# Splitting numbers into two parts: the second part on VectorE alone instead of VectorE or GpSimd

## The chip, the cores and the metric

The kernel runs on one core of a Trainium2 chip. Its time is the device time of one execution in microseconds (us); lower is better. Three runs of the kernel before took 1108.18, 1108.98 and 1110.24 us, so its median is 1108.98 us. In the profile, PE is TensorE's matmuls, PEld its weight loads, DVE is VectorE, ACT is ScalarE, POOL is GpSimd and SP is SyncE, which issues most DMAs.

## What is computed

The reference is a decoder of two layers on one sequence of 1024 positions with 1024 features, in float32. Layer A is gated linear attention; layer B is attention over three dilated windows with shared keys and values. Cut to what matters:

```python
# layer A
q, k, v, g, a_lr = split(x @ w_in)                # 1024 x 3088 weights
log_a = log_sigmoid(a_lr @ w_a2 + b_a2) / 16
o = gla_chunked(q, k, v, log_a)                   # 4 heads, decayed states
o = o * rsqrt(mean(o * o) + eps) * norm_g
x = layer_norm(alpha * x + (o * silu(g)) @ w_out)
# layer B
k, v = split(x @ w_kv); k = rope(k, pos)
q, g = split(x @ w_in); q = rope(q, pos)          # 3 groups x 8 heads of 128
o = softmax-weighted sum over (window, dilation) in ((128,1), (512,4), (2048,16))
x = layer_norm(alpha * x + (o * silu(g)) @ w_out)
```

## The kernel before

**Two parts for each number.** The large products run in TensorE's float32r type, which keeps less of a number than float32. So each operand is held as a high part (a copy rounded to float32r, made on ScalarE by `split_hi`) and a low part (the number less its high part, made by `split_lo`). A product then takes three matmuls: high by high, high by low, low by high. `split_lo` is thus called for every weight and every activation that such a product reads. In the names of the profile `wf` is a weight as loaded, `wh` and `wl` its parts; `woh` and `wol` are those of the last output weights; `xh`, `xl`, `x1h`, `x1l`, `ogh`, `ogl` are parts of activations (of the input, of layer A's result, of the gated attention output); `T` or `tT` are quarter sums of activations and hold both parts.

**Pair jobs.** Most projections of q, k and the queries of layer B go through `pairs` (L777 to L880): two 128-column blocks of weights are multiplied with the activations by a scheme of seven half-size products, P1 to P7, instead of eight. It needs sums of weights (`sum`, with parts in `wh`, `wl` and `s`) and sums of activations (`T`, `tT`). For each job `seven` (L831) copies P1 and P7 out of the accumulator to `u1` and `u2` on ScalarE, and TensorE may start P2, which goes into P1's accumulator, only behind the first copy. Then VectorE adds P6 to `u1`, `c` is `u1` plus the sum of P7 and P4, and `u2` becomes `u1 + u2` (L873 sends it on). In layer B the four quarters of a job are P2's accumulator, `c`, `u2` and `u1`. Each goes through the rotary embedding (`rope`, L1497): `t1` is the quarter times the cosine (VectorE), `t2` two half copies on ScalarE that swap its halves, then times the sine, and `pair` takes `t1 + t2`. The last two may run on VectorE or GpSimd. There are two buffers for `t2`. Layer B has 14 pair jobs: three for the keys and eleven for the queries; the third is the last for the keys, the eighth that for query heads 4 and 5 in the widest window. `xc` is a copy on ScalarE that belongs to turning layer A's result, which goes on beside these jobs (one or two at a job).

**What sets the order.** No instruction is issued as it is written. The code records operations, and a planner (`order`, L270 on) gives each a place by a list schedule with costs for every engine; all are then issued from one line, L469, which is why every row of the profile has this line. `S.vector` binds an operation to VectorE, `S.vp` leaves it to VectorE or GpSimd, `S.va` to VectorE or ScalarE. For such an operation the planner tries both engines and takes the one with the earlier start; an engine is passed over where a cheaper one is free no later:

```python
                    if any(max(free[q], r) <= st and c < o.cost[o.engs.index(e)] for q, c in zip(o.engs, o.cost)):
                        continue

                    key = (max(st, soft), o.prio)
```

So GpSimd gets an operation where the planner thinks VectorE busy. The planner also takes VectorE and GpSimd operations with two inputs in on-chip memory to exclude each other (`shares_port`, L560). Since every choice moves the times of what follows, a change in one choice moves others, on all engines.

Each engine runs its instructions in the planner's order and waits in that order. GpSimd also issues the DMAs that add a low part of weights by accumulation (the rows `DMA wl<-in_w...`).

## Time and profile before

| | |
|---|---|
| median of 3 runs | 1108.98 us (1108.18 to 1110.24) |
| the profiled execution | 1108.76 us |
| its span, first to last instruction | 1107.0 us |
| mean granted clock of TensorE | 0.996 |
| TensorE busy in 490 to 761 us (layer B's pair jobs) | 268.78 of 271.00 us |
| VectorE busy in 490 to 761 us | 223.07 us |
| GpSimd busy in 490 to 761 us | 108.98 us |
| TensorE busy in 761 to 1000 us (attention) | 238.63 of 239.00 us |

The stages in order: the first projections (to 54 us), layer A's pair jobs (54 to 132), linear attention with its value and gate projections (to 360), its output with the layer norm (to 440), layer B's values (from 422) and pair jobs (490 to 761), attention with the gate projections (to 1010), and the output with the layer norm. A row of a group gives engine, operation, output and inputs, count, then busy time in us and the mean in ns of one, then the idle time of the engine just before and what ended it. A row of the timeline gives the start, the duration (of all that a row merges), the engine, the operation and in brackets the idle time before it. A row of stretches gives the length, the busy time of PE, PEld, DVE, ACT and POOL with their counts, the granted clock, the share of DMA and GB/s.

### The profile page before, as it was taken

Reading aid. Unit: us, or ns where it says so; the run is one execution under the profiler, and the core shown is the slowest. Engines: PE = TensorE matmul, PEld = TensorE weight load, DVE = VectorE, ACT = ScalarE, POOL = GpSimd, SP = SyncE. Lnnn points to the kernel's source line nnn. Section 1 sums busy time; section 2 is a strip of 40 time slices with the busy share of each in tenths; the row PEclk is TensorE's granted clock in tenths of the full one; section 3 lists DMA queues with packets and bytes.
Section 4 is the critical chain, followed back from the end, with each engine's and each line's share of the span. In section 5 each row is a group of like instructions: output and inputs, shape, how many; then the busy total and the mean of one; then the engine's idle time right before and its main releaser. Section 6 shows DMA issues by size and latency. Waiting matters only on the chain.

```text
span 1107.0 us, 20264 instructions
## 1 busy us (share of the span) xinstructions
PE 1093.0 (99%) x7532; PEld 933.5 (84%) x7532; DVE 878.1 (79%) x1756; ACT 651.3 (59%) x1326; POOL 263.1 (24%) x281
## 2 busy tenths in 40 slices
PE   9999999999999999999999999999999999999997
PEld 9988888888888888888878888888888888888876
DVE  5886879999567589887877889885688778896588
ACT  5565545666465265656566666665677787663252
POOL 0122100000013021012454254342233554340010
PEclk9999999999999999999999999999999999999999
DMA  8477773144262455856766686679534552341644
GB/s 298 144 210 207 247 286 120 60 146 168 92 210 87 152 169 183 249 167 154 186 161 180 162 216 168 176 188 277 158 106 124 181 166 91 109 152 68 188 137 171
DMA packets 92626, 185.70 MB, mean 168 GB/s; under 512 B 16912, under 2 KB 38032, under 8 KB 92528
## 3 DMA queue, kind: packets, MB, share of 16 engines
q1 hardware_dynamic: 84320, 167.11, 45.2%
q0 software_dynamic: 8208, 17.31, 9.3%
q8 instruction: 59, 0.97, 0.4%
q14 instruction: 39, 0.32, 0.1%
HBM read 134.57 MB, written 47.71 MB: 165 GB/s over the span
## 4 chain that ended last, share of the span: by engine, by line
PE 94%; DVE 2%; DMA 2%; ACT 1%; issue 1%; POOL 0%; DVEq 0%; ACTq 0%; POOLq 0%
PE acc L469 30%; PE sev L469 28%; PE po L469 11%; PE lv L469 9%; PE vac L469 8%; PE ms L469 4%; PE pro L469 3%; DMA wf<-in_wOB 1%; DMA wf<-in_wB 1%; DVE wl L469 0%; ACT wl L469 0%; DVE rt L469 0%; ACT t L469 0%; ACT wh L469 0%; DVE wol L469 0%
## 5 line engine op out<-in xcount | busy, mean ns | idle before, releaser
L469 ACT ACTIVATE wh<-wf 128x1024 fp32r<-128x1024 f32 (+3 forms) x118 | 99.4, 844 | 91.8 <-PE acc L469 34.6
L469 PE MATMUL sev<-T,wh 128*128 128x512 f32 x448 | 137.9, 389 | 0.0
L469 PEld LDWEIGHTS sev<-T,wh 128*128 128x128 f32 x448 | 84.1, 188 | 17.5
L469 PE MATMUL sev<-T,wl 128*128 128x512 f32 x224 | 87.1, 389 | 0.0
L469 DVE TENSOR_TENSOR wl<-wf,wh 128x1024 fp32r<-128x1024 f32 (+3 forms) x56 | 63.4, 1137 | 10.7 <-ACT wh L469 10.4
L469 PE MATMUL lv<-K,Q 128*64 128x64 f32 (+2 forms) x512 | 71.4, 287 | 0.4 <-DVE sts L469 0.4
L469 PE MATMUL acc<-x1h,wh 128*128 128x512 f32 x160 | 71.1, 444 | 0.0
L469 POOL TENSOR_TENSOR wl<-wf,wh 128x1024 fp32r<-128x1024 f32 x6 | 14.3, 2386 | 228.4 <-PE ms L469 192.4
L469 PE MATMUL acc<-x1h,wl 128*128 128x512 f32 x160 | 62.8, 393 | 0.0
L469 PE MATMUL acc<-x1l,wh 128*128 128x512 f32 x160 | 62.5, 391 | 0.0
L469 DVE CUSTOM_DVE_ANT_0 P<-lv,bmask 128x256 f32<-128x256 f32 (+1 forms) x128 | 47.1, 378 | 15.5 <-PE lv L469 11.9
L469 PEld LDWEIGHTS lv<-K,Q 128*64 128x64 f32 (+1 forms) x512 | 51.6, 164 | 8.9 <-DVE sts L469 1.2
L469 ACT ACTIVATE P<-P,sts 128x64 f32<-128x64 f32 (+2 forms) x128 | 50.0, 392 | 13.2 <-DVE sts L469 12.9
L469 POOL DMA_DIRECT2D wl<-in_wB x42 | 37.0, 888 | 80.5 <-ACT wl L469 78.3
L469 DVE TENSOR_TENSOR u<-u,sev 128x512 f32<-128x512 f32 x54 | 36.7, 684 | 21.4 <-PE sev L469 20.9
L469 POOL TENSOR_TENSOR pair<-t,t 128x512 f32<-128x512 f32 x26 | 43.4, 1672 | 42.7 <-DVE t L469 32.0
L469 PE MATMUL acc<-xh,wh 128*128 128x512 f32 x128 | 52.5, 410 | 0.0
L469 ACT ACTIVATE t<-u 64x512 f32<-64x512 f32 x56 | 35.3, 631 | 28.5 <-DVE u L469 17.7
L469 PE MATMUL acc<-xh,wl 128*128 128x512 f32 x128 | 50.1, 391 | 0.0
L469 PE MATMUL acc<-xl,wh 128*128 128x512 f32 x128 | 50.0, 390 | 0.0
L469 PEld LDWEIGHTS sev<-T,wl 128*128 128x128 f32 x224 | 42.0, 188 | 8.7
L469 PE MATMUL acc<-ogh,wh 128*128 128x512 f32 x120 | 47.4, 395 | 0.0
(347 smaller groups left out, 3431.7 us busy)
## 6 DMA issues: line engine op xcount, KB each, us to landing
wf<-in_wB SPq DMA_DIRECT2D x32, 512.0 KB, 6.4
wf<-in_wA SPq DMA_DIRECT2D x24, 512.0 KB, 4.4
qd<-pair SPq DMA_DIRECT2D x22, 512.0 KB, 4.9
Q<-qd SPq DMA_DIRECT2D x22, 512.0 KB, 6.8
wl<-in_wB POOLq DMA_DIRECT2D x33, 256.0 KB, 7.5
wf<-in_wO SPq DMA_DIRECT2D x16, 512.0 KB, 3.4
wf<-in_wOB SPq DMA_DIRECT2D x16, 512.0 KB, 3.5
wf<-in_wV SPq DMA_DIRECT2D x10, 512.0 KB, 3.4
```

The lines of the kernel that those rows point to most:

```text
L469: getattr(handle[o.eng], meth)(*[conv(a) for a in args], **{k: conv(v) for k, v in kw.items()})
```

## The change

One word changes: `split_lo`'s subtraction is bound to VectorE.

```diff
     def split_lo(dst, src, hi):
-        S.vp.tensor_sub(dst, src, hi.bitcast(F32))
+        S.vector.tensor_sub(dst, src, hi.bitcast(F32))
```

Before, 34 of these subtractions were placed on GpSimd: 7 of 128x1024 (6 `wl`, 1 `wol`) and 27 of 128x512 (7 `wl` of sums, 8 `ogl`, 5 `tT`, 3 `T`, 2 `x1l`, and `s` and `sum`). All are on VectorE now. The planner then places other operations anew. GpSimd has 257 instructions instead of 287, VectorE 1780 instead of 1759, ScalarE 1146 instead of 1137. Twelve of the sums `u2 = u1 + u2` stand on GpSimd, where five did. TensorE has the same matmuls, in an order that differs mostly in the pair jobs of layer B and in the attention stage.

**The third pair job of layer B, on GpSimd and VectorE.** In these names `u1`, `u2`, `c`, `t1`, `t2` and `pair` are the rotary work above, `wl<-sum` a split, and the last number only tells buffers apart. GpSimd before:

```order
L469 TENSOR_TENSOR u2_5849<-u1_5843,u2_5849 128x512
L469 TENSOR_TENSOR t2_5965<-t2_5965,sinT_3181 128x512
L469 TENSOR_TENSOR pair_5984<-t1_5960,t2_5955 128x4x16x8
L469 TENSOR_TENSOR pair_5984<-t1_5963,t2_5965 128x4x16x8
L469 DMA wl_6007<-in_wB 128x512
```

GpSimd now:

```order
L469 TENSOR_TENSOR u2_5860<-u1_5853,u2_5860 128x512
L469 DMA wl_5921<-in_wB 128x512
L469 TENSOR_TENSOR pair_5986<-t1_5965,t2_5949 128x4x16x8
L469 DMA wl_6012<-in_wB 128x512
L469 TENSOR_TENSOR pair_5914<-t1_6002,t2_5996 128x4x16x8
```

VectorE before:

```order
L469 TENSOR_TENSOR u1_5843<-u1_5843,sev_5898 128x512
L469 TENSOR_TENSOR wl_5939<-sum_5816,wh_5926 128x512
L469 TENSOR_TENSOR wl_5939<-sum_5832,wh_5926 128x512
L469 TENSOR_TENSOR c_5948<-u1_5843,sev_5796 128x512
L469 TENSOR_TENSOR t1_5960<-c_5948,cosT_2944 128x512
```

VectorE now:

```order
L469 TENSOR_TENSOR u1_5853<-u1_5853,sev_5855 128x512
L469 TENSOR_TENSOR c_5935<-u1_5853,sev_5802 128x512
L469 TENSOR_TENSOR wl_5956<-sum_5846,wh_5940 128x512
L469 TENSOR_TENSOR wl_5956<-sum_5862,wh_5940 128x512
L469 TENSOR_TENSOR t1_5965<-c_5935,cosT_2944 128x512
```

The sine product of `u2` and one `pair` have left GpSimd, and `c` stands ahead of the two splits instead of behind them. None of the two splits was on GpSimd.

**The eighth pair job of layer B, on GpSimd and ScalarE.** GpSimd before:

```order
L469 TENSOR_TENSOR pair_6800<-t1_6783,t2_6785 128x4x16x8
L469 DMA wl_6807<-in_wB 128x512 x2
L469 TENSOR_TENSOR pair_6860<-t1_6850,t2_6839 128x4x16x8
L469 TENSOR_TENSOR pair_6860<-t1_6873,t2_6866 128x4x16x8
L469 DMA wl_6902<-in_wB 128x512
```

GpSimd now:

```order
L469 TENSOR_TENSOR pair_6800<-t1_6785,t2_6783 128x4x16x8
L469 DMA wl_6810<-in_wB 128x512 x2
L469 TENSOR_TENSOR u2_6749<-u1_6743,u2_6749 128x512
L469 TENSOR_TENSOR t2_6867<-t2_6867,sinT_3181 128x512
L469 TENSOR_TENSOR pair_6886<-t1_6862,t2_6857 128x4x16x8
L469 TENSOR_TENSOR pair_6886<-t1_6865,t2_6867 128x4x16x8
L469 DMA wl_6909<-in_wB 128x512
```

ScalarE now, in the same job:

```order
L469 ACTIVATE t2_6857<-c_6850 64x512 x2
L469 ACTIVATE t2_6867<-u2_6749 64x512 x2
L469 ACTIVATE t2_6894<-u1_6743 64x512
L469 ACTIVATE wh_6902<-wf_6816 128x512
L469 ACTIVATE wl_6909<-wf_6816 128x512
L469 ACTIVATE wh_6902<-sum_6896 128x512
L469 ACTIVATE t2_6894<-u1_6743 64x512
L469 ACTIVATE xc_6922<-xb_6841 128x2x256
L469 ACTIVATE u1_6932<-sev_6853 128x512
```

GpSimd has the order here that it had in the third job before, with `u2` and its sine product. ScalarE's rows are those of the third job before too, where the copy `u1` of the next job stood directly behind the last `t2`; now an `xc` stands between. VectorE makes `c` behind the two splits here, as it did in the third job before. From the start of the next job TensorE has 42 matmuls (P1, P7, P5 and half of P6) ahead of P2, as it had behind the third job before. In the fifth pair job `u2`, its sine product and one `pair` stand on GpSimd now as well, with `c` behind two splits on VectorE, and an `xc` ahead of `u1`; the three splits on ScalarE stand ahead of the last two `t2` copies there, and TensorE has 51 matmuls ahead of P2 of the sixth.

**The first pair job of layer A, on TensorE.** In `tT13` the first digit names the sum (1 for P5, 3 for P7) and the second its piece. Before:

```order
L469 MATMUL sev_783<-tT12_656,wl_754 128x512
L469 MATMUL sev_783<-tT13_781,wh_740 128x512 x2
L469 MATMUL sev_783<-tT13_781,wl_754 128x512
L469 MATMUL sev_768<-tT33_788,wh_524 128x512 x2
L469 MATMUL sev_768<-tT33_788,wl_539 128x512
```

Now:

```order
L469 MATMUL sev_786<-tT12_674,wl_753 128x512
L469 MATMUL sev_769<-tT33_784,wh_523 128x512 x2
L469 MATMUL sev_769<-tT33_784,wl_540 128x512
L469 MATMUL sev_786<-tT13_778,wh_741 128x512 x2
L469 MATMUL sev_786<-tT13_778,wl_753 128x512
```

The last piece of P7 stands ahead of the last piece of P5 now. VectorE makes `tT13` ahead of `tT33` in both.

## The prediction

> **What bounds the kernel now.** I read the head of the profile's page first, then TensorE's own waits, then the time around the longest of them.

> ```profile
> span 1107.0 us, 20264 instructions
> ...
> PE 1093.0 (99%) x7532; PEld 933.5 (84%) x7532; DVE 878.1 (79%) x1756; ACT 651.3 (59%) x1326; POOL 263.1 (24%) x281
> ...
> PE 94%; DVE 2%; DMA 2%; ACT 1%; issue 1%; POOL 0%; DVEq 0%; ACTq 0%; POOLq 0%
> ```

> TensorE is busy 99% of the span and holds 94% of the chain that ended last. VectorE at 79% and GpSimd at 24% are off that chain nearly everywhere. So work that moves from GpSimd to VectorE has no price of its own. It has a price, or a gain, only where TensorE waits for something that the move makes earlier or later. TensorE's waits are these:

> ```profile
> PE sev L469 <- ACT u L469: 2.2, 1, 2.2
> PE lv L469 <- issue: 1.4, 2, 1.1
> PE pro L469 <- DVE zero L469: 1.3, 1, 1.3
> PE vac L469 <- issue: 0.7, 1, 0.7
> PE acc L469 <- POOL wol L469: 0.4, 1, 0.4
> PE lv L469 <- DVE sts L469: 0.4, 1, 0.4
> ```

> They sum to 6.4 us. The waits on "issue" name no engine, and the one on `zero` lies at the start, ahead of every operation that moves. Within reach of the change lie the 2.2 (the fourth pair job waits for a copy that ScalarE makes) and the 0.4 (a split on GpSimd). That bounds any gain: no more than some 3 us of waiting, and what the wait costs after itself. The largest costs more than its row says:

> ```profile
> 556.04 0.62 PE L469 MATMUL sev<-T,wh 128*128 128x512 f32 x2
> 556.50 0.39 PE L469 MATMUL sev<-T,wl 128*128 128x512 f32 x1
> 559.10 0.62 PE L469 MATMUL sev<-x1h,wh 128*128 128x512 f32 x1 [2.22 <-ACT u L469]
> ...
> 562.51 0.51 PE L469 MATMUL sev<-x1h,wl 128*128 128x512 f32 x1
> ```

> ```profile
> 559.10:562.60 3.50, 3.50 (x9) 2.72 (x10) 3.50 (x6) 1.74 (x3) 1.28 (x1) 0.53 0.82 131
> ```

> Matmuls start 0.23 us apart before (two in 556.50 - 556.04). The next should have started at 556.73 and started at 559.10: 2.4 us. Behind the gap the granted clock is 0.53 for 3.5 us, and eight matmuls take 562.51 - 559.10 = 3.41 us where they would have taken 8 x 0.23 = 1.84: another 1.6 us. The stall is worth 4.0 us in all.

> **What makes that stall.** It is the rotary work of the third pair job, on three engines (ScalarE, then GpSimd, then VectorE):

> ```profile
> 549.71 1.27 ACT L469 ACTIVATE t<-c 64x512 f32<-64x512 f32 x2 [3.42 <-DVE c L469]
> 551.01 1.27 ACT L469 ACTIVATE t<-u 64x512 f32<-64x512 f32 x2
> 555.45 0.63 ACT L469 ACTIVATE t<-u 64x512 f32<-64x512 f32 x1 [3.16 <-POOL pair L469]
> ...
> 557.80 0.63 ACT L469 ACTIVATE t<-u 64x512 f32<-64x512 f32 x1
> 558.45 1.09 ACT L469 ACTIVATE u<-sev 128x512 f32<-128x512 f32 x2
> ```

> ```profile
> 546.22 1.61 POOL L469 TENSOR_TENSOR u<-u,u 128x512 f32<-128x512 f32 x1
> 552.43 1.29 POOL L469 TENSOR_TENSOR t<-t,sinT 128x512 f32<-128x512 f32 x1 [4.59 <-ACT t L469]
> 553.68 3.44 POOL L469 TENSOR_TENSOR pair<-t,t 128x512 f32<-128x512 f32 x2
> ```

> ```profile
> 544.68 0.69 DVE L469 TENSOR_TENSOR u<-u,sev 128x512 f32<-128x512 f32 x1 [1.55 <-PE sev L469]
> 545.80 3.19 DVE L469 TENSOR_TENSOR wl<-sum,wh 128x512 fp32r<-128x512 f32 x2 [0.44 <-ACT wh L469]
> 548.92 0.67 DVE L469 TENSOR_TENSOR c<-u,sev 128x512 f32<-128x512 f32 x1
> ```

> Read from the end. TensorE waits for `u<-sev` at 558.45. That copy stands in ScalarE's order behind a `t<-u` that could start only at 555.45, when GpSimd had ended a `pair` and so freed a `t` buffer. That `pair` stood behind GpSimd's product with the sine (552.43), which waited for ScalarE's second `t`. The first `t` waited for `c`, and `c` stood on VectorE behind two splits that took 3.19 us, nearly all of it beside GpSimd's `u` at 546.22. VectorE had been brought into step with TensorE at 544.68 (it waited 1.55 us for it), so lateness from before plays no part: it is the order of this one job that costs 4.0 us.

> **The change, part by part.** Operations that leave GpSimd, and their price on VectorE:

> ```profile
> L469 POOL TENSOR_TENSOR wl<-wf,wh 128x1024 fp32r<-128x1024 f32 x6 | 14.3, 2386 | 228.4 <-PE ms L469 192.4 <-ACT wh L469 36.0
> L469 POOL TENSOR_TENSOR wl<-sum,wh 128x512 fp32r<-128x512 f32 x7 | 9.6, 1374 | 4.9 <-ACT wh L469 4.9
> L469 POOL TENSOR_TENSOR wol<-wf,woh 128x1024 fp32r<-128x1024 f32 x1 | 2.4, 2384 | 48.0 <-ACT woh L469 48.0
> ...
> L469 DVE TENSOR_TENSOR wl<-wf,wh 128x1024 fp32r<-128x1024 f32 x45 | 56.4, 1256 | 9.4 <-ACT wh L469 9.2
> L469 DVE TENSOR_TENSOR wol<-wf,woh 128x1024 fp32r<-128x1024 f32 x7 | 8.6, 1223 | 4.2 <-ACT woh L469 4.2
> ...
> L469 ACT ACTIVATE xc<-xb 128x512 uint16<-128x512 uint16 x16 | 12.6, 786 | 0.4 <-DMA xb<-x1p 0.3
> ```

> Of the 34 splits that move, 7 are 1024 wide and 27 are 512 wide. GpSimd loses 14.3 + 2.4 + 9.6 + 20 x 1.37 = 54 us. VectorE gains 7 x 1.25 + 27 x 0.69 (the row at 544.68) = 27 us, less the 7 sums `u` that the planner now gives to GpSimd in exchange (7 x 0.69 = 5). On VectorE's 878 us that is under 3%, and TensorE waits for VectorE's own results only 0.4 us in the middle of the span, so the 22 us lie beside TensorE's matmuls. If that cover were gone in one place, what is late next is the copy or split that TensorE takes there; the four terms below are those places.

> (a) Third pair job. GpSimd no longer takes the sine product of `u`, nor the second `pair`, and VectorE makes `c` ahead of the two splits. Of the chain above, the 3.19 us ahead of `c` and the 1.29 of the sine go. ScalarE's wait of 3.16 us goes with them, which is more than the stall of 2.4 us: **-4.0 us**. Bounds: 0 (something else is late there) and -4.0.

> (b) Eighth pair job. The order that made the stall stands here now, operation for operation: on VectorE `u`, two splits, then `c`; on GpSimd two DMA issues, `u`, the sine product, `pair`, `pair`; on ScalarE the same `t` copies and splits ahead of the copy for the next job. TensorE has as many matmuls to cover it as at 559 (42 from the next job's start to the product that needs the copy). VectorE is again tied to TensorE by its wait ahead of `u`. So the stall of 4.0 us should come again here, where there is none now. One thing is added: an `xc` copy stands ahead of the `u` copy on ScalarE, 786 ns by its group, some 0.6 us of the queue's time. Behind the waiting ScalarE stand the `u` copies, and TensorE waits for these: **+4.6 us**. Bounds: 0 and 4.6 + 0.8, should `xc` itself wait for its DMA.

> [...]

> (c) The split `wol` near the end goes from 2384 to 1223 ns. TensorE's wait for it, 0.4 us, is shorter than the difference: **-0.4 us** if VectorE is free; 0 if not.

> (d) The first pair job. Five splits of the quarter sums move to VectorE while it makes the last of them for TensorE (VectorE, GpSimd, TensorE):

> ```profile
> 39.23 2.38 DVE L469 TENSOR_TENSOR sum<-wf 128x512 f32<-128x512 f32 x2
> ...
> 53.31 1.29 DVE L469 TENSOR_TENSOR wl<-wf,wh 128x512 fp32r<-128x512 f32 x2 [0.97 <-ACT wh L469]
> ...
> 59.66 1.28 DVE L469 TENSOR_TENSOR tT<-xg,tT 128x512 fp32r<-128x512 f32 x2
> ```

> ```profile
> 39.01 1.45 POOL L469 TENSOR_TENSOR tT<-xg,tT 128x512 fp32r<-128x512 f32 x1 [1.46 <-ACT tT L469]
> ```

> ```profile
> 60.66 0.62 PE L469 MATMUL sev<-tT,wh 128*128 128x512 f32 x2
> ...
> 61.34 0.62 PE L469 MATMUL sev<-tT,wh 128*128 128x512 f32 x2
> ```

> The two splits at 59.66 end at 60.3 and 60.94; TensorE takes the first at 60.66 and the second at 61.34. In the new order TensorE takes the second ahead of the first, so it waits 0.3 us even if VectorE keeps its time. Five more operations cost VectorE 5 x 0.64 = 3.2 us; two sums beside GpSimd's split took 2.38 instead of 1.28, so 1.1 us come back; 0.97 us of idle time is there to be used. Ends: 0 and 0.3 + 3.2 - 1.1 - 0.97 = 1.4. I take **+0.3 us**, near the lower end, because the other three GpSimd splits lay beside VectorE too.

> The sum: 1107.0 - 4.0 + 4.6 - 0.4 + 0.3 = 1107.5. The profiled execution took 1108.76 us, 1.8 over its span, and the median of the runs is 0.2 above that: 1107.5 + 1.8 + 0.2 = **1109.5 us**, 0.5 above 1108.98. About 0.2% (2.2 us) is what a measurement of this kernel can tell from no change.

> **The rivals.** *The stall goes and does not come back* (chance 0.22). If GpSimd's `u` in the eighth job starts after VectorE's two splits, `c` comes some 1.9 us earlier (3.19 against 1.29 for two) and most of the gap closes. Then only (a), (c) and (d) stand: 1107.0 - 4.0 - 0.4 + 0.3 = 1102.9, 1104.9 us. For it: the margin is a matter of which engine starts first. Against it: VectorE's splits wait for ScalarE there (0.44 us), while GpSimd's `u` waits only for VectorE's.

> *Two more waits* (chance 0.21), the side of slower. In the fifth pair job GpSimd now also has `u`, the sine product and a `pair` in a row, and VectorE makes `c` behind two splits. TensorE has 51 matmuls of cover in the sixth job, 9 more than at 559, worth 9 x 0.23 = 2.1 us, and ScalarE has an `xc` copy more. The gap there would be 2.4 + 0.6 - 2.1 = 0.9 us, and 1.6 more if the clock goes down: 2.5 us, 1112.0 us in all. It decides as soon as ScalarE's `u` copy is more than 2.1 us later, relative to its job, than at 558.45. Against it: three copies stand ahead of the wait on GpSimd now, and run while it lasts.

> *The port freed* (chance 0.07). VectorE's operations with two inputs run longer beside GpSimd's, as at 545.80 and 39.23. With 54 us of GpSimd's splits gone, VectorE could be early everywhere, so that each wait within reach and the price of the gap go: 2.4 + 1.6 + 0.4 + 0.4 = 4.8 less, 1104.2 us. Against it: in the eighth job GpSimd's own `u` and `pair` are the neighbours, not splits. [...]

> **How the numbers follow.** The forecast (the stall moves) has 0.50; the rivals 0.22, 0.21 and 0.07. The forecast's own range is 1107.6 (no clock loss in (b), 1.6 less, and 0 for (d)) to 1111.8 (0.8 for `xc`, 0.4 for (c), 1.1 more for (d)). The range reaches to the rivals on both sides: 1104.6 to 1112.6. Faster by over 0.2%: the first and third rivals, 0.29, less what falls short, 0.27. Slower by over 0.2%: the second and the upper end of the forecast, 0.27. Between: 0.46.

> **What would show it.** Right: no wait of TensorE for `u` near 556; one of about 3 us for `u` in the eighth pair job, near 655, with granted clock near 0.5 behind it; no wait for `wol`; GpSimd 30 instructions fewer. Wrong: no wait of TensorE over 1 us between 490 and 761 (first rival), two of them (second), or a change of TensorE's waits in the attention stage behind 761, which no term covers since no split is moved there before 970.

## The result, and the profile after

The changed kernel takes 1115.31 us (median of 6 runs, 1113.10 to 1118.03) against 1108.79 us for the kernel before (median of 6 runs). The ratio is 1.0069, with a 95% interval of 1.0055 to 1.0082: it is slower by 0.7%. The prediction was 1109.5 us with a range up to 1112.6, so the time lies outside the range. The profiled execution took 1115.79 us, with a span of 1114.0 us.

From the page of the changed kernel, the span, the engines' busy time and the chain that ended last:

```profile
span 1114.0 us, 20213 instructions
...
PE 1095.3 (98%) x7532; PEld 935.2 (84%) x7532; DVE 881.5 (79%) x1777; ACT 657.8 (59%) x1335; POOL 218.3 (20%) x251
...
PE 84%; DVE 8%; DMA 3%; ACT 2%; issue 2%; POOL 0%; DVEq 0%; SPq 0%; ACTq 0%; POOLq 0%
```

GpSimd lost 30 instructions and 45 us of work, VectorE gained 3.4 us net, where the prediction reckoned with 22. Summed over VectorE's groups, the operations that it gained are worth 27 us at their mean durations of before, but its operations run shorter now by 21 us in all (`s<-sum,s` took 805 ns on average instead of 1278). That was the premise of the third rival, and it did come true (two splits took 3.19 us beside GpSimd's `u` at 545.80 of the kernel before, and 1.28 at 59.66 with GpSimd idle; what makes them longer is not shown), but TensorE's waits did not go with it. TensorE's share of the chain fell from 94% to 84%, and VectorE, off it before, holds 8%. TensorE has the same 7532 matmuls. Its waits, as total, number and longest:

```profile
PE sev L469 <- ACT u L469: 6.6, 3, 4.6
PE vac L469 <- issue: 2.3, 1, 2.3
PE pro L469 <- DVE zero L469: 1.3, 1, 1.3
PE lv L469 <- issue: 1.1, 2, 0.6
```

The waits for `u` went from 2.2 us in one place to 6.6 in three, and the wait on "issue" at `vac` from 0.7 to 2.3. Since the matmuls are as many, the start of the n-th matmul in the one trace less that in the other tells where the 7.0 us of span came from:

| place | us after less before |
|---|---|
| first 42 us | -0.2 |
| first pair job of layer A, 60 to 65 | +1.1 |
| linear attention, 172 to 218 (3.3 of it at the wait at `vac`) | +3.5 |
| 218 to 490 | -0.3 |
| third pair job of layer B, 559 to 563 | -4.1 |
| eighth, 656 to 668 | +7.9 |
| twelfth, 741 | +1.2 |
| attention | -1.0 |
| `wol` | -0.7 |
| after the last matmul | -0.3 |

The stall of the third pair job is gone and stands in the eighth, as the prediction had it, but twice as large. TensorE there, and then the row of stretches from the wait's end (length, busy time of PE, PEld, DVE, ACT, POOL, then the granted clock):

```profile
656.05 0.39 PE L469 MATMUL sev<-T,wl 128*128 128x512 f32 x1
661.07 0.80 PE L469 MATMUL sev<-x1h,wh 128*128 128x512 f32 x1 [4.63 <-ACT u L469]
...
666.36 0.83 PE L469 MATMUL sev<-T,wh 128*128 128x512 f32 x2
```

```profile
661.07:666.60 5.53, 5.53 (x13) 4.37 (x14) 3.10 (x4) 1.07 (x2) 1.27 (x1) 0.50 0.83 203
```

The gap is 4.8 us (661.07 less 656.05 less 0.23). Twelve matmuls behind it take 5.29 us instead of 2.7, and a 13th is slow too: the clock is 0.50 for 5.5 us, where it was 0.53 for 3.5 us behind the stall at 559. ScalarE, VectorE and GpSimd ahead of it:

```profile
643.15 0.59 ACT L469 ACTIVATE t<-sev 64x512 f32<-64x512 f32 x1 [1.39 <-DVE t L469]
643.76 0.64 ACT L469 ACTIVATE wh<-wf 128x512 fp32r<-128x512 f32 x1
...
645.87 1.14 ACT L469 ACTIVATE wh<-sum 128x512 fp32r<-128x512 f32 x2
650.73 1.28 ACT L469 ACTIVATE t<-c 64x512 f32<-64x512 f32 x2 [3.73 <-DVE c L469]
652.03 1.27 ACT L469 ACTIVATE t<-u 64x512 f32<-64x512 f32 x2
656.81 0.63 ACT L469 ACTIVATE t<-u 64x512 f32<-64x512 f32 x1 [3.50 <-POOL pair L469]
...
659.81 0.78 ACT L469 ACTIVATE xc<-xb 128x512 uint16<-128x512 uint16 x1
660.46 1.05 ACT L469 ACTIVATE u<-sev 128x512 f32<-128x512 f32 x2
```

```profile
642.45 0.67 DVE L469 TENSOR_TENSOR t<-sev,cosT 128x512 f32<-128x512 f32 x1
...
644.38 0.68 DVE L469 TENSOR_TENSOR u<-u,sev 128x512 f32<-128x512 f32 x1
646.51 3.53 DVE L469 TENSOR_TENSOR wl<-sum,wh 128x512 fp32r<-128x512 f32 x2 [1.45 <-ACT wh L469]
649.96 0.68 DVE L469 TENSOR_TENSOR c<-u,sev 128x512 f32<-128x512 f32 x1
```

```profile
646.95 1.93 POOL L469 TENSOR_TENSOR u<-u,u 128x512 f32<-128x512 f32 x1
653.45 1.64 POOL L469 TENSOR_TENSOR t<-t,sinT 128x512 f32<-128x512 f32 x1 [4.57 <-ACT t L469]
655.04 2.95 POOL L469 TENSOR_TENSOR pair<-t,t 128x512 f32<-128x512 f32 x2
```

It is the chain of the third job, link by link. Three links are longer than there. VectorE's splits waited 1.45 us for ScalarE's `wh` (0.44 there) and took 3.53 (3.19); GpSimd's sine product took 1.64 (1.29); and the `xc` copy stands ahead of `u`. The `wh` came late because VectorE did: ScalarE's `t` at 643.15, ahead of four copies and `wh`, had waited for VectorE's `t<-sev,cosT` at 642.45. That one started 13.8 us ahead of the time at which TensorE could have gone on (656.28), where the same one in the third job (541.10) was 15.6 us ahead of it (556.73).

The second loss was in no term. TensorE stops in the linear attention at the same place in the program in both kernels (behind the 1112th matmul), before and after:

```profile
174.51 0.39 PE L469 MATMUL vac<-wl,xh 128*128 128x512 f32 x1
175.65 0.40 PE L469 MATMUL vac<-wh,xl 128*128 128x512 f32 x1 [0.75 <-issue]
```

```profile
175.30 0.40 PE L469 MATMUL vac<-wl,xh 128*128 128x512 f32 x1
178.02 0.50 PE L469 MATMUL vac<-wh,xl 128*128 128x512 f32 x1 [2.32 <-issue]
```

```profile
178.69:182.10 3.41, 3.41 (x10) 2.66 (x9) 1.23 (x3) 0.00 (x0) 0.00 (x0) 0.50 0.00 0
```

Behind the longer stop, matmuls start 0.43 us apart instead of 0.23: the clock is halved here as well, for 3.41 us. The gap is 1.6 us longer than before, and the half clock costs another 1.7. The trace has 16 KB packets of a queue called "instruction". Before, one of them starts at 172.68, 2.1 us ahead of the stop. After, none comes in the 5.5 us ahead of it, and one starts at 175.84, 0.3 us behind the stop; TensorE goes on 2.2 us after the packet's start. The trace doesn't say for which engine a packet is; that this one is TensorE's program is taken from its timing. The queue's row, before in 170.0 to 174.74 and after in 175.53 to 178.02 (after has no such row for 170.0 to 175.53):

```profile
q8 instruction: 1, 0.02, 1.8%
```

```profile
q8 instruction: 1, 0.02, 2.4%
```

The third loss is in the first pair job of layer A (VectorE, ScalarE, TensorE of the changed kernel, then SyncE before and after):

```profile
63.15 1.29 DVE L469 TENSOR_TENSOR sum<-wf 128x512 f32<-128x512 f32 x2 [2.23 <-DMA wf<-in_wA]
...
63.88 0.63 ACT L469 ACTIVATE wh<-sum 128x512 fp32r<-128x512 f32 x1 [0.84 <-DVE sum L469]
64.41 1.07 ACT L469 ACTIVATE u<-sev 128x512 f32<-128x512 f32 x2
...
65.05 0.50 PE L469 MATMUL sev<-xh,wh 128*128 128x512 f32 x1 [0.82 <-ACT u L469]
```

```profile
54.03 0.93 SPq L469 DMA_DIRECT2D wf<-in_wA  x2
```

```profile
54.72 0.90 SPq L469 DMA_DIRECT2D wf<-in_wA  x2
```

The weights of the second job are loaded into buffers that two splits on VectorE free. These splits stand behind one more `tT` split now, so the loads are issued 0.7 us later. VectorE's sums wait for them, ScalarE's `wh` waits for a sum, the copy `u` stands behind that `wh`, and TensorE waits for `u`.

### The profile page after: what moved, and what is told of

The parts are those of the page before. It is cut to its first block, busy times and chain, and to the rows that moved or that the text cites. A ratio compares the mean times of both kernels' runs of the same rounds, so it can differ in the third digit from the quotient of the medians.

```text
span 1114.0 us, 20213 instructions
## 1 busy us (share of the span) xinstructions
PE 1095.3 (98%) x7532; PEld 935.2 (84%) x7532; DVE 881.5 (79%) x1777; ACT 657.8 (59%) x1335; POOL 218.3 (20%) x251
## 4 chain that ended last, share of the span: by engine, by line
PE 84%; DVE 8%; DMA 3%; ACT 2%; issue 2%; POOL 0%; DVEq 0%; SPq 0%; ACTq 0%; POOLq 0%
PE acc L469 28%; PE sev L469 21%; PE po L469 12%; PE lv L469 9%; PE vac L469 8%; PE ms L469 3%; PE pro L469 2%; DMA wf<-in_wB 1%; DVE wl L469 1%; DVE t L469 1%; DVE sum L469 1%; DVE pair L469 1%; DVE rt L469 1%; ACT t L469 1%; ACT wh L469 1%
## 5 line engine op out<-in xcount | busy, mean ns | idle before, releaser
L469 ACT ACTIVATE wh<-wf 128x1024 fp32r<-128x1024 f32 (+3 forms) x118 | 99.3, 844 | 107.6 <-PE acc L469 39.1
L469 PE MATMUL sev<-T,wh 128*128 128x512 f32 x448 | 138.2, 390 | 0.0
L469 PEld LDWEIGHTS sev<-T,wh 128*128 128x128 f32 x448 | 84.4, 188 | 17.6
L469 PE MATMUL sev<-T,wl 128*128 128x512 f32 x224 | 87.1, 389 | 0.0
L469 DVE TENSOR_TENSOR wl<-wf,wh 128x1024 fp32r<-128x1024 f32 (+3 forms) x62 | 72.1, 1167 | 10.9 <-ACT wh L469 10.6
L469 PE MATMUL lv<-K,Q 128*64 128x64 f32 (+2 forms) x512 | 71.6, 286 | 0.1
L469 PE MATMUL acc<-x1h,wh 128*128 128x512 f32 x160 | 70.6, 441 | 0.0
L469 DVE CUSTOM_DVE_ANT_0 P<-lv,bmask 128x256 f32<-128x256 f32 (+1 forms) x128 | 47.4, 378 | 20.6 <-PE lv L469 18.9
L469 PE MATMUL acc<-x1h,wl 128*128 128x512 f32 x160 | 62.8, 392 | 0.0
L469 PE MATMUL acc<-x1l,wh 128*128 128x512 f32 x160 | 62.5, 390 | 0.0
L469 PEld LDWEIGHTS lv<-K,Q 128*128 128x128 f32 (+1 forms) x512 | 51.7, 164 | 7.6 <-issue 0.5
L469 ACT ACTIVATE P<-P,sts 128x64 f32<-128x64 f32 (+2 forms) x128 | 49.9, 391 | 12.1 <-DVE sts L469 10.9
L469 DVE TENSOR_TENSOR wl<-sum,wh 128x512 fp32r<-128x512 f32 x54 | 50.7, 967 | 6.6 <-ACT wh L469 6.5
L469 PE MATMUL acc<-xh,wh 128*128 128x512 f32 x128 | 52.7, 411 | 0.0
L469 POOL DMA_DIRECT2D wl<-in_wB x42 | 37.3, 901 | 76.1 <-ACT wl L469 74.6
L469 DVE TENSOR_TENSOR u<-u,sev 128x512 f32<-128x512 f32 x54 | 36.5, 680 | 19.6 <-PE sev L469 19.5
L469 DVE TENSOR_TENSOR t<-t,sinT 128x512 f32<-128x512 f32 x50 | 36.6, 733 | 18.7 <-ACT t L469 18.3
L469 PE MATMUL sev<-x1h,wh 128*128 128x512 f32 x112 | 45.1, 403 | 5.8 <-ACT u L469 5.8
L469 PE MATMUL acc<-xh,wl 128*128 128x512 f32 x128 | 50.1, 391 | 0.0
L469 PE MATMUL acc<-xl,wh 128*128 128x512 f32 x128 | 49.9, 390 | 0.0
L469 PEld LDWEIGHTS sev<-T,wl 128*128 128x128 f32 x224 | 42.1, 188 | 8.8
L469 POOL TENSOR_TENSOR pair<-t,t 128x512 f32<-128x512 f32 x24 | 36.2, 1513 | 61.8 <-DVE t L469 50.5
```

The costliest lines, as they stand in the source:

```text
L469: getattr(handle[o.eng], meth)(*[conv(a) for a in args], **{k: conv(v) for k, v in kw.items()})
```

## The experiments

All but one edit the list of operations that the planner hands on (`done`, behind L469): an operation goes to another place in the list, or to the other engine at its old place, and nothing is planned anew. So the matmuls can be compared one by one with those of the kernel that was edited. The numbers are those of the recorded operations. The helpers:

```python
def ahead(done, a, b):      # a is issued directly ahead of b
def behind(done, a, b):     # a is issued directly behind b
def to_vector(done, *n):    # these run on VectorE
```

Each ratio is to runs of the kernel before on the same chip (medians 1106.91, 1107.83 and 1107.14 us for the three groups of runs).

**Splits moved, order kept.** The kernel before, with its own order:

```diff
+def edit(done):
+    for o in done:
+        meth, args, kw = o.calls[0]
+        if o.eng == "POOL" and meth == "tensor_sub" and args[2].steps and args[2].steps[-1][0] == "bitcast":
+            o.eng = "DVE"
+    return done
```

> The order of the kernel before on every engine, and only the engine of the 34 splits changed from GpSimd to VectorE, each at its old place in the order. Theory (what costs is the new order that the planner makes, not the splits themselves): the wait near 559 stays (2.2 us and 1.6 of clock), the wait for wol goes, the first pair job gains up to 1.1 us: 1108 to 1110 us, no difference from before that can be measured. Rival (VectorE's added 27 us reach TensorE): new waits of TensorE for VectorE in many places, 1112 us or more.

Measured: 1111.78 us, ratio 1.0050 (1.0035 to 1.0065). That is 4.9 us over the kernel before on its chip, the size that the rival gave. The stall (here at 563) stays and the wait for `wol` goes, but there are 5.5 us more in the profiled execution, in many places: 0.7 in the first 50 us, 1.7 at 82, 0.8 in 500 to 540, 0.9 at 736, 0.7 near 980. The largest, on TensorE and on VectorE ahead of it:

```profile
81.94 0.50 PE L469 MATMUL sev<-xh,wh 128*128 128x512 f32 x1 [1.42 <-ACT u L469]
```

```profile
77.80 0.75 DVE L469 TENSOR_SCALAR mn<-z,par 128x512 f32<-128x512 f32 x1 [3.61 <-DMA mq<-c]
```

So the splits on VectorE do cost TensorE time when nothing else moves, and the step of the prediction that laid those 22 us beside TensorE's matmuls fails for this order. But it isn't VectorE's load that reaches TensorE. VectorE's busy time is 879.8 us, 1.7 more than before, and ahead of the largest wait it stands idle for 3.61 us, until a DMA has landed that was issued at 69.54, some 8 us earlier (the same one took 8.3 us from issue to landing in the kernel before). The same `mn` waited 0.48 us for ScalarE there; why it waits for that DMA here stays open. At 736 two splits that were on VectorE all along take 3.20 us beside GpSimd's `u` instead of 2.59. What the move shifts at such places is when operations meet.

**Splits back on GpSimd, new order kept.** The counterpart: the changed kernel, with the 34 splits on GpSimd at their places in the new order.

```diff
+def edit(done):
+    for o in done:
+        if o.seq in BACK:        # the 34 splits that were on GpSimd before
+            o.eng = "POOL"
+    return done
```

> The order of the changed kernel on every engine, and only the engine of the 34 splits put back to GpSimd, each at its place in that order: the counterpart of the run with the old order and the splits on VectorE, which was 4.9 us slower than before. Theory (the new order costs by itself): the gaps at 178, 661 and 741 stay, wol's wait comes back, ratio to before 1.006 to 1.008. Rival (VectorE's added work costs by itself, as in the old order): the gap at 65 goes, others shrink, ratio 1.002 to 1.004.

Measured: 1124.36 us, ratio 1.0154 (1.0133 to 1.0174), far above both expectations. The gaps at 65, 665 and 745 are still there, and new ones have come. Three rows of TensorE's waits:

```profile
PE sev L469 <- ACT u L469: 8.1, 6, 4.8
PE lv L469 <- issue: 2.7, 2, 2.0
...
PE acc L469 <- POOL wol L469: 1.1, 1, 1.1
```

Each order fits its own engines. The old order loses 0.5% with the splits on VectorE, and the new one loses a further 0.8% (1.0154 against 1.0069) with the splits on GpSimd. So what the change costs can't be shared out between "the splits" and "the order": the planner makes an order for the engines it is given, and the two results differ by where each leaves a wait.

**The third pair job alone.** The kernel before, with `c` ahead of the two splits there:

```diff
+def edit(done):
+    ahead(done, 2520, 2480)      # c of the third job, its first split
+    return done
```

> The kernel before with one move: in the third pair job of layer B, VectorE makes c ahead of the two splits, as it does in the changed kernel; nothing else differs. Theory (term a of the prediction, the order of this one job costs 4.0 us): no wait near 559, full clock behind it, 4.0 us less than before, 1104.8 us. Rival (the gain of the changed kernel at 559 came from the sine product and pair that left GpSimd there): a gap of 1 us or more stays, gain under 2 us.

Measured: 1105.15 us, ratio 0.9989 (0.9980 to 0.9998). In the profiled execution the gap at 559 is gone whole, half clock and all: 4.1 us at that place. The medians differ by 1.8 us only, for two reasons. A wait of 0.8 us for `u` came near 728, and the half clock behind a wait of 2.2 us doesn't follow in every execution (below). The runs of the kernel before bear this out: 18 of the 21 on this chip had a mean granted clock of 0.998 or 0.999, where the profiled execution with its half clock had 0.996.

**The eighth pair job, link by link.** Three runs of the changed kernel with one move each.

```diff
+    ahead(done, 2960, 2920)      # VectorE: c ahead of the two splits
```

> The changed kernel with one move: in the eighth pair job of layer B, VectorE makes c ahead of the two splits instead of behind them. Theory (the chain c, t, sine product, pair, t, u is what TensorE waits for at 661): c starts near 645 instead of 650, the copies t start 3.1 us earlier (then GpSimd's u2 sets them), TensorE's gap goes from 4.6 to about 1.5 us and the half clock behind it (6.8 us long, some 3 us lost) goes with it: 6 us less, about 1109.3 us. Rival (ScalarE is late there because of its own copies and xc): the gap stays above 4 us and the time at 1115.

```diff
+    to_vector(done, 2970)        # the sine product of u2 on VectorE
```

> The changed kernel with one operation on another engine: the product of the second t with the sine in the eighth pair job is on VectorE, not on GpSimd; c stays behind the splits. Theory: GpSimd starts its first pair near 652.8 instead of 655.0, so the t copy that waits for it and all behind it come 2.2 us earlier; TensorE's gap goes from 4.6 to about 2.4 us, the half clock from two pieces of 3.4 us to one (1.5 us less lost): 3.7 us less, about 1111.6 us. Rival (ScalarE late by its own work): unchanged, 1115 us.

```diff
+    ahead(done, 3021, 2978)      # ScalarE: the next job's u1 ahead of the t that waits for the pair
```

> The changed kernel with one move on ScalarE: the copy u1 of the ninth pair job of layer B stands ahead of the t copy that waits for GpSimd's pair, not behind it. Theory (TensorE waits at 661 only because u1 stands in ScalarE's order behind that t): the gap of 4.6 us is gone wholly and no half clock follows, where an earlier c and an earlier pair each left 2.2 to 2.4 us; 7.5 us less than the changed kernel, level with the kernel before (ratio 0.999 to 1.001). Rival (the copy of P1 is itself late, or the t copies that are now 1 us later make the next job wait): a gap of 1 us or more here or near 680.

Measured: 1110.86 us with `c` first (ratio 1.0037, 1.0025 to 1.0049), 1109.60 with the sine product moved (1.0018, 1.0006 to 1.0030), 1109.56 with `u1` ahead (1.0015, 1.0005 to 1.0024), against 1.0069 for the changed kernel. By these ratios they are 3.5, 5.6 and 6.0 us below it, where 6, 3.7 and 7.5 were expected. At the place itself the profiled executions gave 5.1, 5.3 and 3.7 us. TensorE in the first and in the second:

```profile
656.23 0.50 PE L469 MATMUL sev<-x1h,wh 128*128 128x512 f32 x1 [2.20 <-ACT u L469]
```

```profile
660.13 0.50 PE L469 MATMUL sev<-x1h,wh 128*128 128x512 f32 x1 [2.02 <-ACT u L469]
```

Each shortens the chain by some 2.5 us, and in these executions no half clock followed what was left. The profiled one of the first was the fastest of six, with a granted clock of 0.998; the other five had 0.996 or 0.997. In the third the wait at P2 is gone, but the next product waits instead (TensorE, then ScalarE):

```profile
655.33 0.39 PE L469 MATMUL sev<-x1h,wl 128*128 128x512 f32 x1
657.68 1.06 PE L469 MATMUL sev<-T,wh 128*128 128x512 f32 x2 [1.96 <-ACT u L469]
```

```profile
649.92 0.60 ACT L469 ACTIVATE u<-sev 128x512 f32<-128x512 f32 x1
...
657.06 0.57 ACT L469 ACTIVATE u<-sev 128x512 f32<-128x512 f32 x1
```

`u1` is copied at 649.92, but `u2` still stands behind the `t` copies and comes at 657.06, and P4 needs P7's accumulator free. So the cause is shown: both `u` copies stand in ScalarE's order behind a `t` that waits for GpSimd's `pair`. With both ahead of it the gap is gone (the run with all places, below).

**The stop at 178.** The changed kernel, with the small `lv` products one group (three `vac` matmuls) earlier, where they were before:

```diff
+    ahead(done, 800, 936)        # TensorE: lv<-q,k and lv<-X ahead of one vac group
```

> The changed kernel with one move on TensorE: in the linear attention the small products lv stand one group of three vac matmuls earlier, as in the kernel before. Theory (at 178 TensorE waits for its next piece of program; its fetch starts where TensorE is some way into the lv products, and behind the weights wf if these start first): the fetch starts about 2 us ahead of the halt as before, the gap goes from 2.5 to 1.1 us or less, no half clock behind it: 1.5 to 3 us less than the changed kernel, ratio to before 1.004 to 1.0055. Rival (the gap is chance, or hangs on what VectorE does): gap 1.8 to 2.9 as in the three runs of that order.

Measured: 1112.34 us, ratio 1.0040 (1.0024 to 1.0055). The wait is 0.8 us, the packet starts 1.9 us ahead of the stop again, and no half clock follows: 3.1 us less at that place than in the profiled run of the change. Over all profiles, the seven executions with `lv` at its old place have gaps (over the usual interval) of 0.4 to 1.0 us here, the six with `lv` at its new place 1.1, 1.1, 1.8, 2.5, 2.6 and 2.9. At the old place the packet starts 1.3 to 2.1 us ahead of the stop; at the new place 1.3 us ahead in the two with 1.1, and between 0.5 us ahead and 0.7 us behind in the other four. What holds it up in these four stays open. The load of `wf` had begun ahead of the packet in all four, in one of them by 0.1 us only, but so it had in one of the two with 1.1.

**All places at once, on the changed kernel.**

```diff
+    behind(done, 319, 424)       # one tT split behind the two wl<-wf, first pair job of layer A
+    ahead(done, 800, 936)
+    for u1, u2, p7, t in ((3021, 3026, 3025, 2978), (3371, 3376, 3375, 3333)):
+        behind(done, u1, p7)     # eighth and twelfth job: u1 and u2 of the next job
+        behind(done, u2, u1)     # ahead of the t that waits for the pair
+        behind(done, t, u2)
```

> The changed kernel with four local moves, no new planning: (1) first pair job of layer A: the two splits of wf on VectorE ahead of one tT split, so that their buffers come free 0.5 us earlier; (2) the lv products one group of vac earlier on TensorE; (3) and (4) in the eighth and in the twelfth pair job of layer B, both copies u1 and u2 of the next job on ScalarE ahead of the t copy that waits for a pair. Theory (the four places hold what the changed kernel lost): gap at 65 from 1.0 to about 0.4, at 178 to 1.1 or less, at 661 none (and none behind it, since u2 is ahead too, where u1 alone left 2.1 us at the next product), at 741 none; 0.5 + 3.1 + 7.9 + 1.2 us less than the profiled run of the changed kernel, so some 5 below the kernel before: ratio 0.995 to 0.997. Rival (each gap that closes opens another): ratio 0.999 or more, with new gaps of 1 us in other places.

> The changed kernel itself once more, on the same chip as the two runs beside it. Theory: gaps at 65, 178, 661 and 741 in their places again; at 661 4 to 5 us; at 178 anything from 1.1 to 2.9 us with or without half clock behind it, which makes the spread of its times; ratio to before 1.0055 to 1.008.

Measured: 1107.46 us with the moves, ratio 0.9999 (0.9987 to 1.0010); 1114.56 us for the changed kernel again, ratio 1.0063 (1.0048 to 1.0078). Against the profile of the latter the four places give 1.1, 1.6, 7.1 and 1.6 us, 11.3 in all. They hold all that the change lost and more. But 4.5 us come back in new waits at 674, 700, 712 and 749, all in pair jobs behind the eighth. Four rows of TensorE's waits with the moves:

```profile
PE sev L469 <- ACT u L469: 2.1, 2, 1.2
...
PE vac L469 <- issue: 0.8, 1, 0.8
PE sev L469 <- DMA wl<-in_wB: 0.6, 1, 0.6
PE sev L469 <- DVE u L469: 0.5, 1, 0.5
```

The rival of that run was right: each gap that closes opens others. TensorE comes to the later jobs sooner and waits there for `u`, for weights and for VectorE.

**A version that beats both.** The kernel before, with the same kinds of move. First `c` ahead of the splits in the third and the twelfth job, and `wol` on VectorE:

```diff
+    ahead(done, 2520, 2480)
+    ahead(done, 3315, 3275)
+    to_vector(done, 5369)
```

> The kernel before with three local edits and no new planning: c ahead of the two splits in the third and in the twelfth pair job of layer B, and the one wol split of GpSimd on VectorE. Theory: no gap at 559, none near 730 (0.3 to 0.9 us there), none for wol near 1057 (0.6): 1.2 us below the kernel with the first edit alone, which had a ratio of 0.9989; so 0.997 to 0.998. Rival (each gap that closes opens the next one, as 0.9 us came near 727 when the one at 559 went): 0.999 to 1.000.

```diff
+    for u1, u2, p7, t in ((2581, 2586, 2585, 2538), (3371, 3376, 3375, 3333)):
+        behind(done, u1, p7)
+        behind(done, u2, u1)
+        behind(done, t, u2)
+    to_vector(done, 5369)
```

> The kernel before with local moves, no new planning: in the third and in the twelfth pair job of layer B both copies u1 and u2 of the next job on ScalarE ahead of the t copy that waits for a pair; c stays behind the splits in both; the one wol split of GpSimd on VectorE. Theory: the gaps at 559 and near 728 are gone both, since nothing that TensorE needs stands behind a wait for a pair any more; the run with c moved in both had 0.9975 and a gap of 1.2 near 728, so 0.996 to 0.997. Rival (the t copies, 1.1 us later, delay VectorE's pairs and with them the jobs behind): a gap of 1 us or more in a later job, 0.9975 or more.

Measured: 1105.01 us, ratio 0.9975 (0.9965 to 0.9984), and 1104.27 us, ratio 0.9973 (0.9963 to 0.9982). In the first a wait of 1.0 us for `u` near 728 stays, because in the twelfth job VectorE makes the `pair` itself, behind the splits that `c` has passed; ScalarE's `t` waits 4.05 us for it. In the second no wait for `u` is left at all. Its profiled execution was the slowest of twelve (1106.10 us), with half clock behind the wait of 1.7 us (granted clock 0.63 in 294 to 298 us). TensorE's waits there, complete:

```profile
PE lv L469 <- issue: 1.9, 2, 1.7
PE pro L469 <- DVE zero L469: 1.3, 1, 1.3
PE vac L469 <- issue: 0.8, 1, 0.8
PE lv L469 <- DVE sts L469: 0.4, 1, 0.4
```

## Why the prediction was wrong, point by point

**The bound on what is within reach failed first.** It set the waits on "issue" aside because they name no engine. One of them came to cost 3.3 us more, 1.6 of waiting and 1.7 of clock. The order of TensorE itself had changed by one group of matmuls just ahead of it, and with that order the next 16 KB packet came later, closer to the stop or behind it. The run with `lv` put back shows that link; what holds the packet up is not shown.

**(a) Third pair job: right in mechanism, in size by luck of the execution.** -4.0 us predicted, -4.1 in the profiles, and `c` alone closes the gap. But 1.6 us of the term are half clock, which the profiled execution of the kernel before had; by their granted clock (0.998 or more), 43 of its 67 later runs had not. Between medians `c` alone brought 1.8 us, with 0.8 us lost to a new wait.

**(b) Eighth pair job: the mechanism was right, the size was not.** +4.6 predicted (bound 5.4), +7.9 measured. The step that failed is that lateness from before plays no part, since VectorE's wait for TensorE ahead of `u` ties the two. That wait, 1.55 us in the third job, isn't there in the eighth: VectorE came late. It had almost caught up at `u`, but ScalarE, which had waited for an earlier `t` of VectorE, had not, and VectorE's splits waited 1.0 us longer for ScalarE's `wh`. Why VectorE was late stays open. With slower splits and a slower sine product (0.3 each) and `xc` (0.65) the gap was 4.8 us instead of 3.0. The price of a gap was also mis-sized: it was taken from one case as 1.6 us, and behind this longer gap the half clock lasted twice as long (6.83 us against 3.41), at a cost of some 3 us. The lower end of the forecast's range took no loss of clock behind a gap of 3.0 us, 1.6 us less. No run shows that: all five waits of 2.7 us or more, over all profiles, had half clock behind them.

**(c) `wol`: right in kind.** -0.4 predicted, -0.7 measured at that place, in the changed kernel and in the last two versions.

**(d) First pair job: right in sign, wrong in mechanism.** +0.3 predicted from the order of two matmul groups and VectorE's time, +1.1 measured. No wait of TensorE stands at those groups. The term followed VectorE's results and not the buffers that its instructions free; the loads behind those buffers were what came late. Putting the splits back in front closed the gap.

**What no term covered:** the twelfth pair job (+1.2), where the second rival looked at the fifth instead; and -1.0 in attention, where the order differs but no split moves.

**That VectorE's added time is hidden** was taken from its 79%. Most of that time never came up, since other operations ran shorter, and yet the move costs 4.9 us in the medians of the old order. In the new order the planner had moved other work around it, and what was left is in the table above.

The sum was thus a balance of terms of 4 us each with opposite signs. In the spans it gave 1107.5 us, and 1114.0 were measured. One term was 3.3 us too small and another 3.3 us at `vac` were missing, which is the miss of 6.5; what else was off cancels. The stated range began at 1104.6 us, just above the third rival's 1104.2, which changes nothing here.

## What to carry to other kernels

Where a list scheduler places everything, the price of binding an operation to an engine is not the operation's time: it is which waits the new order leaves, and these are a few places of 1 to 8 us each. They can be found by lining up the two traces by the n-th instruction of the bound engine, and mended by moving single operations in the finished list: this gave 0.27% over the kernel before, where the change lost 0.7%. The first thing to look for is a copy that the bound engine needs (`u` here) queued on another engine behind an instruction that waits for a third.

## What the runs showed of the hardware

**A packet of the queue "instruction" starts close to TensorE's stop.** These packets of 16 KB start 27 to 35 us apart among the large matmuls of layer B's pair jobs (505 to 745 us of the changed kernel), and 3.3 to 11.2 us apart in 175 to 223, where the small ones begin. At the stop near 178 TensorE went on 2.2 to 3.0 us after the packet's start in every profile (3.0 in the kernel before, 2.2 in the changed one), and stood still for what of this lay behind the stop: 0.4 to 2.9 us at this one packet. That TensorE waited for the packet is the author's estimate from these times; no trace names the engine that a packet is for.
